# A transfer-bound matmul with adapted weights: first pair rounded by ScalarE, m merged earlier, half loads, an earlier first store, and idle waits on VectorE

## Chip, cores, metric

One core of a Trainium2 chip. The metric is device microseconds of a whole execution; medians are quoted with the lowest and highest run. The "span" is the part of an execution from its first to its last profiled instruction; it is a little shorter than the time.

## The reference

```python
batch, seq_len, in_dim, out_dim, rank = 16, 2048, 256, 256, 16
W_adapted = W + scale * (lora_A @ lora_B)
W_norm = np.sqrt(np.sum(W_adapted ** 2, axis=0, keepdims=True) + 1e-8)
W_final = W_adapted / W_norm * m
y = x.reshape(-1, in_dim) @ W_final          # 32768 x 256 in, 32768 x 256 out, float32
```

x and y are 33.6 MB each, the weights 0.3 MB. There is one matmul per row of x, so the work is mostly moving bytes.

## The kernel before

x is cut into 8 blocks of 4096 rows (4.19 MB, 32 KB per partition); five block buffers fit on the chip. A block is 8 chunks, two chunks are a pair. A pair goes: GpSimd rounds it to bf16, TensorE transposes it, VectorE copies the transposed pair out, TensorE multiplies it by w_final, ScalarE copies each chunk's result back *into the buffer of x*, and ScalarE's queue stores it. Loads go out on SyncE's queue (q1 in the profile), stores on ScalarE's (q10).

The parts that the change touches:

```python
loads = [(0, 2), (2, 2), (4, CH - 4)] + units[1 : XBUFS - 1]        # (first chunk, chunks)
loads += [((XBUFS - 1) * CH, CH - 3)]                               # chunks 32-36: 20 KB rows
loads += [(XBUFS * CH - 3 + c, 1) for c in range(3)] + units[XBUFS:]  # 37, 38, 39: 4 KB rows
...
stores = [(b * CH, CH, 21 + b) for b in range(F - 1)]               # (.., .., issued behind chunk)
stores += [(G - CH, CH // 2, 24), (G - CH // 2, CH // 2, 24)]
FIRST = len(stores)
stores += [(G + c, 1, G + 3) for c in range(4)]                     # 4 KB rows
stores += [(G + 4, CH - 4, 47)]
stores += [(b * CH, CH, max(47, (b + 1) * CH - 1)) for b in range(F + 1, NBLK - 1)]
...
# GpSimd: the first cast waits for dve 4; before pair REST it waits for half of block 2's store
if p == 0:
    nc.gpsimd.wait_ge(sem("dve"), 4)
if p == REST:
    nc.gpsimd.wait_ge(sem(f"store{HALF}"), 16)
...
for _ in range(IDLE):                       # 8, at the end of GpSimd's program
    nc.gpsimd.wait_ge(sem("ident"), 1)
...
# TensorE: norm's matmuls, then the one that spreads m over the partitions, then
turned(0)
nc.tensor.wait_ge(dv, 8)                    # w_final is there
nc.tensor.sem_inc(sem("room"), 2)           # two output buffers are free
with nc.Fori(0, NPR // 2, 1, engines=[PE], head_slot={PE: 128}):
    turned(1); product(0); turned(0); product(1)
```

## Time and profile before

| | before |
|---|---|
| time (first 3 runs) | 162.68 us (162.39 to 162.74) |
| span of the profiled run | 161.3 us |
| busiest compute engine | TensorE, 59% |
| bytes, mean rate | 67.42 MB, 418 GB/s |
| first store issued | 48.5 us |
| last arithmetic, last store issued | 131.2, 132 us |

The page and the table of stretches are shown in the prediction. In the table of stretches the columns are: the stretch and its length, busy time (and count) of each engine, the clock granted to TensorE (1 is full), DMA share, GB/s. In short stretches the last two are rough, since a packet counts by where it starts; where I give a loss in microseconds below, it is a sum over the trace's own DMA packet records, each packet's bytes spread over its duration, of how far half-microsecond slices under 424 GB/s fall short of 431. Such a loss comes from the one profiled run of a kernel, while times and mean spans come from all of its runs.

### The profile page before, as it was taken

To read this page: it belongs to the slowest core of one execution; us is meant where nothing else is said; L and a number is where in the kernel's file an instruction comes from. 1 tells how busy PE (TensorE), PEld (TensorE's weight loads), DVE (VectorE), ACT (ScalarE), POOL (GpSimd) and SP (SyncE) were. 2 spreads that over 40 slices of the span, in tenths; PEclk is the share of its full clock that TensorE was granted. 3 is DMA by queue.
4 is the path that set the end of the run, shared out by engine and by line. 5 is a ranking of instruction groups with operands and counts; after the bars stand their busy time and mean duration, and the time that the engine had idled before them with its cause. 6 is when DMAs were issued, how large, how long until landed. Compare 5 with 4: busy or idle time off the path is not lost. (4 is left out here: it accounts for less than half of the span.)

```text
span 161.3 us, 2012 instructions
## 1 busy us (share of the span) xinstructions
PE 95.2 (59%) x786; PEld 83.8 (52%) x786; DVE 46.6 (29%) x44; ACT 63.9 (40%) x67; POOL 62.9 (39%) x39
## 2 busy tenths in 40 slices
PE   0491899999999700000199999999999940000000
PEld 0160799999998600000179989989899930000000
DVE  0439635353635300000033535353445300000000
ACT  3010076868686520000027675856776850000000
POOL 1085339776764000000674479198676200000000
PEclk9999999999999995555559999999999998555555
DMA  4999999999899999989999999999999999999995
GB/s 163 427 455 459 390 504 406 390 488 423 374 412 361 511 423 390 473 374 451 427 482 414 386 463 421 407 433 433 422 484 419 406 479 414 400 479 423 386 443 228
DMA packets 4356, 67.42 MB, mean 418 GB/s; under 512 B 625, under 2 KB 642, under 8 KB 1666
## 3 DMA queue, kind: packets, MB, share of 16 engines
q1 hardware_dynamic: 2160, 33.82, 49.5%
q10 hardware_dynamic: 2194, 33.59, 48.7%
q14 instruction: 2, 0.02, 0.0%
HBM read 33.85 MB, written 33.55 MB: 418 GB/s over the span
## 5 line engine op out<-in xcount | busy, mean ns | idle before, releaser
L256 ACT COPY x_sb<-y_ps 128x1024 f32<-128x1024 f32 x64 | 62.0, 1014 | 60.0 <-PE y_ps L316 57.8
L197 POOL CAST xb<-x_sb 128x2048 bf16<-128x2048 f32 x32 | 60.4, 1900 | 61.3 <-DMA out_dram<-x_sb 27.7
L316 PE MATMUL y_ps<-w_final,xt 128*128 128x256 bf16 x512 | 63.6, 278 | 1.2 <-PEq L291 1.1
L238 DVE COPY xt<-xt_ps 128x1024 f32<-128x1024 f32 x32 | 39.2, 1224 | 72.6 <-PE xt_ps L302 72.6
L316 PEld LDWEIGHTS y_ps<-w_final,xt 128*128 128x128 bf16 x512 | 51.1, 100 | 8.5 <-issue 1.9
L302 PE MATMUL xt_ps<-identity,xb 128*128 128x128 f32 x264 | 37.0, 287 | 28.2 <-PEq L291 28.2
L302 PEld LDWEIGHTS xt_ps<-identity,xb 128*128 128x128 f32 x264 | 31.7, 148 | 30.3 <-issue 30.0
L283 PE MATMUL y_ps<-sq,ones 128*128 128x256 f32 x4 | 2.1, 674 | 1.6 <-DVE sq L223 1.6
L272 PE MATMUL y_ps<-identity,a_nat 128*16 128x128 f32 x2 | 0.6, 394 | 4.1 <-DMA a_nat<-in_lora_A_dram 4.1
L248 ACT ACTIVATE norm<-y_ps,eps_col 128x256 f32<-128x256 f32 x1 | 0.5, 473 | 5.8 <-PE y_ps L283 5.8
L234 DVE TENSOR_TENSOR w_final<-wam,rnorm 128x256 bf16<-128x256 f32 x2 | 2.5, 1266 | 0.0
L283 PEld LDWEIGHTS y_ps<-sq,ones 128*128 128x128 f32 x4 | 1.2, 326 | 2.3 <-DVE sq L223 2.1
L272 PEld LDWEIGHTS y_ps<-identity,a_nat 128*16 128x16 f32 x2 | 0.1, 88 | 4.1 <-issue 4.1
L246 ACT ACT_TABLE_LOAD x1 | 1.3, 1283 | 2.4 <-issue 2.4
L203 POOL MEMSET xb<- 128x2048 bf16 x1 | 1.8, 1804 | 0.7 <-PE xt_ps L302 0.7
L231 DVE RECIPROCAL rnorm<-norm 128x256 f32<-128x256 f32 x1 | 1.7, 1747 | 0.0
L225 DVE COPY m_all<-y_ps 128x256 f32<-128x256 f32 x1 | 0.4, 424 | 3.3 <-PE y_ps L288 3.3
L214 DVE CAST b_bf<-b_nat 16x256 bf16<-16x256 f32 x1 | 0.3, 281 | 3.5 <-DMA b_nat<-in_lora_B_dram 3.5
L288 PE MATMUL y_ps<-m_row,ones 1*128 1x256 f32 x2 | 1.2, 706 | 0.0
L276 PE MATMUL y_ps<-b_bf,aT 16*128 16x256 bf16 x2 | 0.6, 404 | 0.7 <-DVE aT L216 0.7
L219 DVE SCALAR_TENSOR_TENSOR wa<-y_ps,w_nat 128x512 f32<-128x512 f32 x1 | 0.7, 692 | 0.8 <-PE y_ps L276 0.8
L288 PEld LDWEIGHTS y_ps<-m_row,ones 1*128 1x128 f32 x2 | 0.5, 308 | 0.6 <-issue 0.6
(13 smaller groups left out, 3.3 us busy)
## 6 DMA issues: line engine op xcount, KB each, us to landing
x_sb<-in_x_dram SPq DMA_DIRECT2D x5, 4096.0 KB, 26.5
out_dram<-x_sb ACTq DMA_DIRECT2D x5, 4096.0 KB, 22.7
out_dram<-x_sb ACTq DMA_DIRECT2D x5, 2048.0 KB, 29.0
x_sb<-in_x_dram SPq DMA_DIRECT2D x3, 2048.0 KB, 31.4
x_sb<-in_x_dram SPq DMA_DIRECT2D x1, 2560.0 KB, 44.8
x_sb<-in_x_dram SPq DMA_DIRECT2D x2, 1024.0 KB, 6.1
out_dram<-x_sb ACTq DMA_DIRECT2D x4, 512.0 KB, 50.1
x_sb<-in_x_dram SPq DMA_DIRECT2D x3, 512.0 KB, 46.4
```

The lines of the kernel that those rows point to most:

```text
L197: nc.gpsimd.tensor_copy(out=xb_bufs[p % NXB][:], in_=x_bufs[b % XBUFS][:, 2 * c * J : 2 * (c + 1) * J, :],).then_inc(sem("rounded"), 1)
L203: nc.gpsimd.memset(xb_bufs[NPR % NXB][:], 0.0).then_inc(sem("rounded"), 1)
L219: nc.vector.scalar_tensor_tensor(out=wa[:], in0=ab_ps, scalar=float(scale), in1=w_nat[:], op0=ALU.mult, op1=ALU.add).then_inc(dv, 1)
L231: nc.vector.reciprocal(out=rnorm[:], in_=norm[:]).then_inc(dv, 1)
L234: i = nc.vector.tensor_mul(out=w_final[:, t], in0=wam[:, t], in1=rnorm[:])
L238: nc.vector.tensor_copy(out=xt_bufs[p % NXT][:].rearrange("p r t -> p (r t)").bitcast(FP32), in_=xt_ps[p % 2][:],).then_inc(sem("copied"), 1)
L246: nc.scalar.activation(out=warm[:], in_=eps_col[:], func=AF.Sqrt)
L256: nc.scalar.copy(out=x_bufs[b % XBUFS][:, c * J : (c + 1) * J, :], in_=y_ps[g % 2][:]).then_inc(sem("room"), 1)
L283: i = nc.tensor.matmul(n2_ps, ones[:], sq[:, t, :], start=(t == 0), stop=(t == KC - 1))
L288: nc.tensor.matmul(mb_ps, ones[0:1, :], m_row[:], start=True, stop=True).then_inc(pe, 1)
L302: i = nc.tensor.transpose(xt_ps[p % 2][:, j * P : (j + 1) * P], xb_bufs[p % NXB][:, j, :].bitcast(FP32), identity[:],)
L316: i = nc.tensor.matmul(y_ps[h][:, j, :], xt_bufs[p % NXT][:, r : r + P, t], w_final[:, t, :], start=(t == 0 and (j % (J // 2)) == 0), stop ...
```

## The change

Its intent: start computing earlier (m merged before the norm is ready, ScalarE rounds the first pair, GpSimd kept off VectorE's port while w_final is made), wait less for loads (half loads), and begin the stores earlier (behind chunk 19). Idle waits on VectorE were added to those on GpSimd. The core of the diff:

```diff
+    loads = [(0, 2, 2 * J), (2, 2, 2 * J)] + [(g0, 4, 4 * J) for g0 in range(4, 24, 4)]
+    loads += [(24, CH, CH * J), (H - CH, 5, 5 * J), (H - 3, 3, J)]
+    loads += [(H, CH, CH * J)] + [(g0, 4, 4 * J) for g0 in range(H + CH, NCH, 4)]
+    stores = [(b * CH, CH, CH * J, 19 + b) for b in range(F - 1)]
+    stores += [(G - CH, 4, 4 * J, G - 1), (G - 4, 4, 4 * J, G - 1)]
+    stores += [(G, 4, J, G + 3), (G + 4, CH - 4, (CH - 4) * J, 48)]      # pieces share a semaphore
 ... (GpSimd)
-        if p == 0:
-            nc.gpsimd.wait_ge(sem("dve"), 4)
+        if p == 1:
+            nc.gpsimd.wait_ge(sem("dve"), 6)
+        if p == 2:
+            nc.gpsimd.wait_ge(sem("dve"), 8)
 ... (VectorE)
-    nc.vector.wait_ge(sem("pe"), 4)
+    nc.vector.wait_ge(sem("pe"), 3)
     nc.vector.tensor_copy(out=m_all[:], in_=mb_ps).then_inc(dv, 1)
 ...
+    nc.vector.wait_ge(dv, 8)
+    nc.vector.sem_inc(sem("room"), 2)
 ...
     for _ in range(IDLE):
         nc.gpsimd.wait_ge(sem("ident"), 1)
+        nc.vector.wait_ge(sem("ident"), 1)
 ... (ScalarE)
+    wait_load(nc.scalar, 0)
+    nc.scalar.copy(out=xb_bufs[0][:], in_=x_bufs[0][:, 0 : 2 * J, :]).then_inc(sem("early"), 1)
 ... (TensorE: m's matmul moves ahead of the norm's)
-    nc.tensor.wait_ge(dv, 8)
-    nc.tensor.sem_inc(sem("room"), 2)
```

More of the change, by code (lines that the diff above doesn't have):

```diff
@@ L103, with pieces @@
     units += [(NCH - CH, CH // 2), (NCH - CH // 2, CH // 2)]
-    loads = [(0, 2), (2, 2), (4, CH - 4)] + units[1 : XBUFS - 1]
-    loads += [((XBUFS - 1) * CH, CH - 3)]
-    loads += [(XBUFS * CH - 3 + c, 1) for c in range(3)] + units[XBUFS:]
-    load_of = {g: n for n, (g0, cnt) in enumerate(loads) for g in range(g0, g0 + cnt)}
     F = NBLK - XBUFS
     G = F * CH
-    stores = [(b * CH, CH, 21 + b) for b in range(F - 1)]
-    stores += [(G - CH, CH // 2, 24), (G - CH // 2, CH // 2, 24)]
-    FIRST = len(stores)
-    stores += [(G + c, 1, G + 3) for c in range(4)]
-    stores += [(G + 4, CH - 4, 47)]
-    stores += [(b * CH, CH, max(47, (b + 1) * CH - 1)) for b in range(F + 1, NBLK - 1)]
-    stores += [(g0, cnt, g0 + cnt - 1) for g0, cnt in units[-2:]]
-    HALF = FIRST - 2
+    H = XBUFS * CH
+    loads = [(0, 2, 2 * J), (2, 2, 2 * J)] + [(g0, 4, 4 * J) for g0 in range(4, 24, 4)]
+    loads += [(24, CH, CH * J), (H - CH, 5, 5 * J), (H - 3, 3, J)]
+    loads += [(H, CH, CH * J)] + [(g0, 4, 4 * J) for g0 in range(H + CH, NCH, 4)]
+    load_of = {g: n for n, (g0, cnt, _) in enumerate(loads) for g in range(g0, g0 + cnt)}
+    stores = [(b * CH, CH, CH * J, 19 + b) for b in range(F - 1)]
+    stores += [(G - CH, 4, 4 * J, G - 1), (G - 4, 4, 4 * J, G - 1)]
+    FIRST = len(stores)
+    stores += [(G, 4, J, G + 3), (G + 4, CH - 4, (CH - 4) * J, 48)]
+    stores += [(b * CH, CH, CH * J, max(48, (b + 1) * CH - 1)) for b in range(F + 1, NBLK - 1)]
+    stores += [(g0, cnt, cnt * J, g0 + cnt - 1) for g0, cnt in units[-2:]]
+    def pieces(entry):
+        return 16 * (entry[1] * J // entry[2])
     late = [nc.alloc_semaphore(f"store{n}") for n in range(FIRST, len(stores))]
@@ L132, in sem, with transfer, wait_load, wait_store @@
         return sems[name]
-    def in_sbuf(g0, cnt):
+    def transfer(engine, name, entry, dram, store):
+        g0, cnt, rows = entry[:3]
         b, c = divmod(g0, CH)
-        return x_bufs[b % XBUFS][:, c * J : (c + cnt) * J, :]
-    def in_dram(dram, g0, cnt):
         (u0, ucnt), = [u for u in units if u[0] <= g0 < u[0] + u[1]]
         unit = dram[u0 * J * P : (u0 + ucnt) * J * P].rearrange("(p j) k -> p j k", p=P)
-        return unit[:, (g0 - u0) * J : (g0 - u0 + cnt) * J, :]
+        for r in range(0, cnt * J, rows):
+            here = x_bufs[b % XBUFS][:, c * J + r : c * J + r + rows, :]
+            there = unit[:, (g0 - u0) * J + r : (g0 - u0) * J + r + rows, :]
+            src, dst = (here, there) if store else (there, here)
+            engine.dma_start(out=dst, in_=src).then_inc(sem(name), 16)
     def load_x(n):
-        nc.sync.dma_start(
-            out=in_sbuf(*loads[n]), in_=in_dram(x_flat, *loads[n])
-        ).then_inc(sem(f"load{n}"), 16)
+        transfer(nc.sync, f"load{n}", loads[n], x_flat, False)
     def store_y(n):
-        nc.scalar.dma_start(
-            out=in_dram(out_flat, *stores[n][:2]), in_=in_sbuf(*stores[n][:2])
-        ).then_inc(sem(f"store{n}"), 16)
+        transfer(nc.scalar, f"store{n}", stores[n], out_flat, True)
+    def wait_load(engine, g):
+        engine.wait_ge(sem(f"load{load_of[g]}"), pieces(loads[load_of[g]]))
+    def wait_store(engine, n):
+        engine.wait_ge(sem(f"store{n}"), pieces(stores[n]))
     nc.sync.dma_start(
@@ L162 @@
     for n in range(len(loads)):
-        if loads[n][0] == XBUFS * CH:
-            for k in range(HALF + 1):
-                nc.sync.wait_ge(sem(f"store{k}"), 16)
-        if loads[n] == units[-1]:
-            nc.sync.wait_ge(sem(f"store{HALF + 1}"), 16)
+        if loads[n][0] == H:
+            for k in range(FIRST - 1):
+                wait_store(nc.sync, k)
+        if loads[n][0] == H + G - 4:
+            wait_store(nc.sync, FIRST - 1)
         load_x(n)
@@ L183 @@
     ).then_inc(sem("ident"), 1)
-    for p in range(NPR):
+    for p in range(1, NPR):
         b, c = divmod(p, PRB)
         for g in (2 * p, 2 * p + 1):
-            if g == 0 or load_of[g - 1] != load_of[g]:
-                nc.gpsimd.wait_ge(sem(f"load{load_of[g]}"), 16)
-        if p == 0:
-            nc.gpsimd.wait_ge(sem("dve"), 4)
+            if g == 2 or load_of[g - 1] != load_of[g]:
+                wait_load(nc.gpsimd, g)
+        if p == 1:
+            nc.gpsimd.wait_ge(sem("dve"), 6)
+        if p == 2:
+            nc.gpsimd.wait_ge(sem("dve"), 8)
         if p == REST:
-            nc.gpsimd.wait_ge(sem(f"store{HALF}"), 16)
+            wait_store(nc.gpsimd, FIRST - 2)
         if p >= NXB:
@@ L203 @@
     nc.gpsimd.memset(xb_bufs[NPR % NXB][:], 0.0).then_inc(sem("rounded"), 1)
-    for _ in range(IDLE):
-        nc.gpsimd.wait_ge(sem("ident"), 1)
     dv = sem("dve")
@@ L241 @@
         ).then_inc(sem("copied"), 1)
+    for _ in range(IDLE):
+        nc.gpsimd.wait_ge(sem("ident"), 1)
+        nc.vector.wait_ge(sem("ident"), 1)
     nc.scalar.wait_ge(dv, 1)
     nc.scalar.activation(out=warm[:], in_=eps_col[:], func=AF.Sqrt)
-    nc.scalar.wait_ge(sem("pe"), 3)
+    wait_load(nc.scalar, 0)
+    nc.scalar.copy(out=xb_bufs[0][:], in_=x_bufs[0][:, 0 : 2 * J, :]).then_inc(
+        sem("early"), 1
+    )
+    nc.scalar.wait_ge(sem("pe"), 4)
     nc.scalar.activation(
@@ L258 @@
         ).then_inc(sem("room"), 1)
-        due = [n for n in range(len(stores)) if stores[n][2] == g]
+        due = [n for n in range(len(stores)) if stores[n][3] == g]
         if due:
@@ L279 @@
     i.then_inc(pe, 1)
+    nc.tensor.wait_ge(sem("load_m"), 16)
+    nc.tensor.matmul(mb_ps, ones[0:1, :], m_row[:], start=True, stop=True).then_inc(pe, 1)
     nc.tensor.wait_ge(dv, 4)
@@ L286 @@
     i.then_inc(pe, 1)
-    nc.tensor.wait_ge(sem("load_m"), 16)
-    nc.tensor.matmul(mb_ps, ones[0:1, :], m_row[:], start=True, stop=True).then_inc(pe, 1)
     def take(name):
@@ L298, in turned @@
     def turned(p):
-        take("rounded")
         for j in range(2 * J):
@@ L323, in product @@
             i.then_inc(sem("product"), 1)
+    nc.tensor.wait_ge(sem("early"), 1)
     turned(0)
-    nc.tensor.wait_ge(dv, 8)
-    nc.tensor.sem_inc(sem("room"), 2)
     with nc.Fori(0, NPR // 2, 1, engines=[PE], head_slot={PE: 128}):
+        take("rounded")
         turned(1)
         product(0)
+        take("rounded")
         turned(0)
@@ L338 @@
     tc.compile()
-    for s in late:
-        nc.sync.wait_ge(s, 16)
+    for k, s in enumerate(late):
+        nc.sync.wait_ge(s, pieces(stores[FIRST + k]))
         nc.sync.sem_clear(s)
```

## The prediction

> **What bounds the kernel now.** I read the page's slices first, then the table of stretches, then the chain of waits, and only then the timeline of the head.
>
> The page (busy time of PE, the DMA slices, the queues):
>
> ```profile
> PE 95.2 (59%) x786; PEld 83.8 (52%) x786; DVE 46.6 (29%) x44; ACT 63.9 (40%) x67; POOL 62.9 (39%) x39
> DMA  4999999999899999989999999999999999999995
> GB/s 163 427 455 459 390 504 406 390 488 423 374 412 361 511 423 390 473 374 451 427 482 414 386 463 421 407 433 433 422 484 419 406 479 414 400 479 423 386 443 228
> DMA packets 4356, 67.42 MB, mean 418 GB/s; under 512 B 625, under 2 KB 642, under 8 KB 1666
> q14 instruction: 2, 0.02, 0.0%
> ```
>
> No compute engine is over 59% busy, while the DMA row is full except in the first and the last slice. The 67.42 MB are compulsory: x once in, y once out, plus the small weights. The table of stretches gives the rate that counts as full:
>
> ```profile
> core 0: us, PE busy (x) PEld busy (x) DVE busy (x) ACT busy (x) POOL busy (x), PEclk, DMA share, GB/s
> 0.00:3.00 3.00, 0.00 (x0) 0.00 (x0) 0.17 (x2) 0.59 (x1) 0.70 (x6) 1.00 0.25 58
> 3.00:43.00 40.00, 32.45 (x244) 27.64 (x245) 19.45 (x20) 18.52 (x21) 22.82 (x12) 1.00 1.01 432
> 43.00:49.50 6.50, 6.50 (x62) 6.01 (x61) 3.67 (x3) 4.42 (x6) 5.01 (x3) 1.00 0.99 418
> 49.50:52.50 3.00, 2.90 (x28) 2.48 (x26) 1.22 (x1) 2.40 (x3) 0.67 (x1) 1.00 1.02 340
> 52.50:78.00 25.50, 3.12 (x28) 2.42 (x25) 1.22 (x1) 3.19 (x4) 0.12 (x1) 0.66 1.01 435
> 78.00:110.00 32.00, 29.46 (x245) 26.45 (x246) 12.25 (x10) 18.63 (x20) 21.95 (x12) 0.89 1.01 432
> 110.00:158.00 48.00, 20.82 (x189) 18.78 (x187) 8.57 (x7) 16.17 (x17) 11.64 (x7) 0.77 1.00 431
> 158.00:161.30 3.30, 0.00 (x0) 0.00 (x0) 0.00 (x0) 0.00 (x0) 0.00 (x0) 0.50 0.44 189
> ```
>
> Last column: 432 GB/s with loads alone (3 to 43 us), 435 with stores alone (52.5 to 78), 432 with both (78 to 110). So it doesn't matter to the rate which way the bytes go. The time is start-up (about 2.6 us lost in 0:3), 67.42 MB / 432 GB/s = 156.1 us, and a tail (3.3 us at 189 GB/s, so 1.9 us lost). That makes 160.6 of the 161.3 us. The one other hole is 49.5 to 52.5 us: 340 GB/s although the DMA share says 1.02, so the engines are occupied but slow. It costs 3.0 x (432-340)/432 = 0.64 us.
>
> The chain of waits shows the same thing from the other end; its last two pieces are
>
> ```profile
> 130.19 1.01 ACT x_sb L256
> 131.21 0.92 ACTq L262
> ```
>
> The last arithmetic ends at 131.2 us, the last store is issued about 132, and 29 us of stores queued before it still have to drain. Even the middle is elastic; from the list of waits:
>
> ```profile
> POOL xb L197 <- DMA out_dram<-x_sb: 27.7, 1, 27.7
> ```
>
> GpSimd stands 27.7 us by design, until a store has landed, and no byte is moved later for it.
>
> **What the Trainium skill says.** "DMA: Bandwidth & Descriptors", section "Where 436 GB/s comes from", puts the ceiling of the 16 ports at 435.2 GB/s. The trace agrees (432 to 435 above); the same section's HBM limit of about 358 per core doesn't bind here, and the measurement decides. The same page, "Queues, rings and completion order", says that each DMA engine takes turns between queue rows packet by packet. The trace agrees: between 84 and 100 us, with 32 KB load rows (q1) beside 4 KB store rows (q10), the queues moved
>
> ```profile
> q1 hardware_dynamic: 207, 6.26, 90.6%
> q10 hardware_dynamic: 207, 0.78, 11.9%
> ```
>
> exactly as many packets each, so the row size sets the share. "SBUF — State Buffer", section "SBUF: two separate sides", says that VectorE operations with two SBUF inputs and GpSimd operations that read SBUF lock each other out of a shared port pair. The head of the timeline agrees:
>
> ```profile
> 11.30 0.76 DVE L228 TENSOR_TENSOR wam<-wa,m_all 128x256 f32<-128x256 f32 x2
> 11.97 1.75 DVE L231 RECIPROCAL rnorm<-norm 128x256 f32<-128x256 f32 x1
> 13.76 2.45 DVE L234 TENSOR_TENSOR w_final<-wam,rnorm 128x256 bf16<-128x256 f32 x2
> 13.82 2.11 POOL L197 CAST xb<-x_sb 128x2048 bf16<-128x2048 f32 x1 [2.43 <-DMA x_sb<-in_x_dram]
> ```
>
> The two products for w_final take 2.45 us under a GpSimd cast, the same operation for wam took 0.76 with GpSimd idle.
>
> **The change, part by part.** (1) The head. The matmul that spreads m moves ahead of the norm's matmul, so VectorE's copy of m and wam (0.42 + 0.76 us) are done by about 8.8 us, while TensorE sums squares. The reciprocal can start when the norm is ready (9.69 + 0.47 = 10.2 us, was 11.97): 1.8 us earlier. GpSimd's third cast must now wait for w_final, so its two products should take about 0.8 us, not 2.45: 1.7 us more. ScalarE rounds the first pair meanwhile (2,048 elements at twice the 1,014 ns of its 1,024-element copies, about 2 us, from 6.6 us on), before the norm needs it. w_final is then ready about 12.7 us instead of 16.2, and the first product starts near 14.3 us instead of 18.6: about 4 us earlier.
>
> (2) Half loads. Compute runs at 2.62 us per pair of chunks, so 10.5 us per block, beside 9.7 us per load; it stood idle for blocks 1 and 2 (2.8 and 1.4 us before the casts). Halves land about 4.9 us earlier for their first rows, so these waits mostly go.
>
> (3) First store behind chunk 19, one pair (2.62 us) before 21. With (1) and (2) it should be issued about 40 to 43 us instead of 48.5. At 41 us some (41-2.6) x 0.432 = 16.6 of the 21.3 MB of the first loads are in. So the three 4 KB-row loads (chunks 37 to 39), which now run alone from 48 to 53 us, will run beside 32 KB store rows. What this is worth: by the trace's own packet records, which I summed because no view prints them, their 384 packets take 183 ns on average when alone (up to 220 late in the hole), and the 4 KB stores beside big loads take 159. (183-160) x 384 / 16 engines = 0.55 us, the same hole as the 0.64 us above. This is the gain.
>
> (4) The price of halves: blocks 1, 2 and 6 go from 384 packets of 32 KB (1,214 ns by the same records) to 768 of 16 KB (611 ns). 384 x (1222-1214) / 16 = 0.19 us, and about 0.03 us for three more completions.
>
> (5) The idle waits for VectorE stand at the end of a program that has 30 us to spare: 0. They can only shift when instructions are fetched (two packets on q14); the records show each at 0.31 us on one DMA engine, so at most some 0.3 us in the tail.
>
> So the 4 us of the head and all compute gains lie under the DMA and are worth nothing directly; they only bring the first store forward. Sum: -0.55 to -0.64 + 0.22 = about -0.35 us: 162.68 becomes 162.3. I say 162.35, as the hole may not close fully.
>
> **The rivals.** (a) The DMA runs dry in the middle. Before the second group of stores, which now waits for chunk 48, only all loads (33.85 MB) and 3.5 blocks of stores (14.68 MB) exist: 48.5 MB, or about 2.6 + 112.3 = 115 us. Before, chunk 47 released the group at 110.85 us, with GpSimd 3.25 us idle for block 6. Now its first half comes some 5 us sooner; I expect 107 to 110 us. A spare of 5 us speaks against it. If the group came as late as 120, the loss would be 4 to 5 us (167).
>
> (b) Early stores choke the first loads: 32 KB store rows against 20 KB and 4 KB load rows leave these 38% and 11% of the engines. Chunks 32 to 39 then land at 60 us and later. But GpSimd stands at chunk 30 until the first half of block 2 is stored (about 76 to 78 us) anyway, so it is hidden: 0, at worst 1 us.
>
> (c) The gain of 4 us at the head carries to the end: about 158.7. Against it speak the 29 us of queued stores.
>
> (d) The tail. The 16 engines end together only if they share work evenly; in the completion counts of the last store the median engine lands at 160.0 us and the last at 161.2. A longer mixed phase can change this by 0.5 us either way, the largest doubt in my range.
>
> **Range and chances.** 162.35, and 8 times in 10 within 161.7 to 163.1: the lower end has the hole closed, the price zero and a tail 0.3 shorter, the upper end no gain, the full price and a tail 0.3 longer. The runs before spread over 0.35 us. A gain of 2% (3.25 us) would need more than all that is lost at the hole and the tail together: 1%. A loss of 2% needs rival (a): 2%. Within 2%: 97%.
>
> **What would show it.** Right: bytes unchanged, all stretches from 3 to 158 us at 430 or more with no 340 left; first store issued near 41 us, and stores in the packets while loads still run; w_final near 12.7 us with its two products under 1 us; the second group issued before 112 us; the last arithmetic some us before 131, or as late, without effect. Wrong: a stretch of a microsecond or more with a low DMA share around 110 to 120 us (rival a), a slow stretch that has merely moved to other 4 KB rows, or a tail much over 1.9 us lost (rival d).

## The result, and the profile after

| | before | after |
|---|---|---|
| time | 162.43 us (162.24 to 162.74, 6 runs) | 163.57 us (163.27 to 163.90, 6 runs) |
| ratio | | 1.0069 (1.0053 to 1.0086) |
| span of the profiled run | 161.3 us | 162.0 us |
| time less span, mean | 1.29 to 1.31 us in every group of runs | 1.64 us |

The change made the kernel 1.1 us slower; the prediction was 0.35 us faster, with 163.1 as the upper end. From the page after:

```profile
PE 95.3 (59%) x786; PEld 84.7 (52%) x786; DVE 45.0 (28%) x44; ACT 65.9 (41%) x68; POOL 60.9 (38%) x38
DMA  4999999999899999999999999999999999999995
DMA packets 4788, 67.42 MB, mean 416 GB/s; under 512 B 673, under 2 KB 690, under 8 KB 1714
```

The same bytes, the same engines, the same full DMA row. The table of stretches after has the slow stretch in another place:

```profile
3.00:40.00 37.00, 32.64 (x245) 28.06 (x246) 17.96 (x21) 20.60 (x22) 20.80 (x11) 0.95 1.01 432
...
44.50:48.50 4.00, 3.29 (x30) 3.14 (x31) 1.23 (x1) 2.33 (x3) 4.00 (x3) 1.00 1.03 345
48.50:78.00 29.50, 4.76 (x44) 4.09 (x42) 2.45 (x2) 4.47 (x5) 0.25 (x1) 0.62 1.01 430
...
118.00:158.00 40.00, 14.11 (x130) 12.85 (x127) 5.43 (x5) 11.56 (x12) 6.82 (x4) 0.70 1.00 432
158.00:162.00 4.00, 0.00 (x0) 0.00 (x0) 0.00 (x0) 0.00 (x0) 0.00 (x0) 0.50 0.51 217
```

345 GB/s from 44.5 to 48.5 us. The hole was not closed, it went along with the first store. The timelines of ScalarE's queue have that store's issue, before:

```profile
48.53 0.37 ACTq L149 DMA_DIRECT2D out_dram<-x_sb  x1
```

and after:

```profile
42.80 0.37 ACTq L145 DMA_DIRECT2D out_dram<-x_sb  x1
```

In both kernels the loads slow down about 2 us after this issue and stay slow for about 2 us, until the first packets of the store appear (52.6 us before, 47.1 after). The stretches before and after:

```profile
50.50:52.50 2.00, 1.90 (x18) 1.50 (x17) 1.22 (x1) 1.77 (x2) 0.00 (x0) 1.00 1.01 305
```

```profile
45.00:47.00 2.00, 1.79 (x17) 1.72 (x18) 0.69 (x1) 0.93 (x1) 2.00 (x3) 1.00 0.83 215
```

By the packet records the stretch cost 0.69 us before and 0.95 after: after, it fell among loads with 20 KB rows, whose packets took 877 ns on average instead of 766, while the 4 KB rows now took 160 as predicted.

The head did what the prediction said. Timeline after:

```profile
6.59 1.90 ACT L261 CAST xb<-x_sb 128x2048 bf16<-128x2048 f32 x1 [2.72 <-DMA x_sb<-in_x_dram]
10.19 1.75 DVE L235 RECIPROCAL rnorm<-norm 128x256 f32<-128x256 f32 x1 [1.29 <-ACT norm L265]
11.98 0.76 DVE L238 TENSOR_TENSOR w_final<-wam,rnorm 128x256 bf16<-128x256 f32 x2
13.90 3.74 POOL L205 CAST xb<-x_sb 128x2048 bf16<-128x2048 f32 x2 [2.96 <-DMA x_sb<-in_x_dram]
14.45 3.23 PE L332 MATMUL y_ps<-w_final,xt 128*128 128x256 bf16 x16 [2.12 <-PEq L308]
```

w_final is ready at 12.74 us (predicted 12.7, before 16.2) because its two products take 0.76 us with GpSimd held back (2.45 before), and the first product starts at 14.45 us (predicted 14.3, before 18.6). None of it reaches the end. The list of waits and the chain after:

```profile
POOL xb L205 <- DMA out_dram<-x_sb: 29.9, 1, 29.9
```

```profile
131.27 1.01 ACT x_sb L273
132.28 0.92 ACTq L279
```

GpSimd gives 2.2 us of its lead back at the store that it waits for by design (27.7 us before), and the last arithmetic comes a microsecond later than before, with 29 us of stores still to drain.

Two numbers are to be explained, then: 0.7 to 0.8 us more in the span, and about 0.35 us more outside it.

### The profile page after: what moved, and what is told of

It is laid out like the page before. It is cut to its first block, busy times and chain, and to the rows that moved or that the text cites. A ratio compares the mean times of both kernels' runs of the same rounds, so it can differ in the third digit from the quotient of the medians.

```text
span 162.0 us, 2018 instructions
## 1 busy us (share of the span) xinstructions
PE 95.3 (59%) x786; PEld 84.7 (52%) x786; DVE 45.0 (28%) x44; ACT 65.9 (41%) x68; POOL 60.9 (38%) x38
## 2 busy tenths in 40 slices
DMA packets 4788, 67.42 MB, mean 416 GB/s; under 512 B 673, under 2 KB 690, under 8 KB 1714
## 3 DMA queue, kind: packets, MB, share of 16 engines
q1 hardware_dynamic: 2592, 33.82, 49.6%
q10 hardware_dynamic: 2194, 33.59, 48.4%
## 5 line engine op out<-in xcount | busy, mean ns | idle before, releaser
L205 POOL CAST xb<-x_sb 128x2048 bf16<-128x2048 f32 x31 | 58.4, 1896 | 64.3 <-DMA out_dram<-x_sb 29.9
L332 PE MATMUL y_ps<-w_final,xt 128*128 128x256 bf16 x512 | 64.3, 281 | 3.2 <-PEq L308 3.2
L318 PEld LDWEIGHTS xt_ps<-identity,xb 128*128 128x128 f32 x264 | 32.4, 150 | 29.7 <-issue 29.1
L261 ACT CAST xb<-x_sb 128x2048 bf16<-128x2048 f32 x1 | 1.9, 1899 | 2.7 <-DMA x_sb<-in_x_dram 2.7
L232 DVE TENSOR_TENSOR wam<-wa,m_all 128x256 f32<-128x256 f32 x2 | 0.8, 422 | 0.0
```

What stands on the lines that cost most here:

```text
L205: nc.gpsimd.tensor_copy(out=xb_bufs[p % NXB][:], in_=x_bufs[b % XBUFS][:, 2 * c * J : 2 * (c + 1) * J, :],).then_inc(sem("rounded"), 1)
L261: nc.scalar.copy(out=xb_bufs[0][:], in_=x_bufs[0][:, 0 : 2 * J, :]).then_inc(sem("early"), 1)
L318: i = nc.tensor.transpose(xt_ps[p % 2][:, j * P : (j + 1) * P], xb_bufs[p % NXB][:, j, :].bitcast(FP32), identity[:],)
L332: i = nc.tensor.matmul(y_ps[h][:, j, :], xt_bufs[p % NXT][:, r : r + P, t], w_final[:, t, :], start=(t == 0 and (j % (J // 2)) == 0), stop ...
```

## The experiments

Theories at the start. *Inside the span:* the loss belongs to the first store and moves with it, larger among larger load rows; rivals: the half loads cost it, or it is a price of first touching the output, or the 4 KB rows are slow by themselves, as I had predicted. *Outside the span:* the idle waits on VectorE; rival: they are free.

All results in one table. "First store" is the issue of the first one in the profiled run (in e4 of the first big one), "loss there" the loss at that store, "later" the losses at later places where loads and stores meet. Rows marked * have no slow stretch at the first store; their 0.18 or 0.19 is only the three loads with 4 KB rows, which run alone at some 408 GB/s.

| kernel | first store us | loss there | later | span, mean of runs | time less span | ratio to before |
|---|---|---|---|---|---|---|
| before | 48.5 | 0.69 | 0.05 | 161.1 to 161.3 | 1.29 to 1.31 | 1 |
| after | 42.8 | 0.95 | 0 | 161.95 | 1.64 | 1.0069 |
| e1 | 43.0 | 1.09 | 0 | 161.9 | 1.56 | 1.0059 (1.0045 to 1.0073) |
| e2 | 45.3 | 1.29 | 0 | 161.9 | 1.62 | 1.0056 (1.0042 to 1.0069) |
| e3 | 47.9 | 0.92 | 0 | 161.3 | 1.44 | 1.0010 (0.9997 to 1.0023) |
| e4 | 48.4 | 0.90 | 0 | 161.5 | 1.30 | 1.0011 (0.9998 to 1.0024) |
| e5 | 45.3 | 1.04 | 0.20 | 161.75 | 1.31 | 1.0029 (1.0012 to 1.0045) |
| e6* | 49.6 | 0.18 | 0.29 | 161.2 | 1.57 | 1.0015 (0.9997 to 1.0034) |
| e7 | 47.6 | 0.70 | 0 | 161.25 | 1.30 | 0.9994 (0.9978 to 1.0010) |
| e8 | 21.1 | 0.19 | 0.79 | 161.55 | 1.31 | 1.0017 (1.0000 to 1.0034) |
| e9* | 49.8 | 0.18 | 0.49 | 161.3 | 1.56 | 1.0025 (1.0011 to 1.0039) |
| e10* | 49.6 | 0.19 | 0.65 | 161.6 | 1.30 | 1.0032 (1.0009 to 1.0055) |
| e11* | 50.9 | 0.18 | 1.15 | 161.8 | 1.59 | 1.0052 (1.0037 to 1.0066) |
| e12 | 42.5 | 0.99 | 0 | 161.8 | 1.65 | 1.0061 (1.0046 to 1.0077) |
| e13* | 49.5 | 0.19 | 0.48 | 161.3 | 1.57 | 1.0030 (1.0014 to 1.0046) |
| e14 | 48.1 | 0.85 | 0 | 161.3 | 1.31 | 1.0014 (0.9999 to 1.0029) |
| e15 | 46.1 | 0.92 | 0 | 161.8 | 1.30 | 1.0042 (1.0029 to 1.0056) |
| e16* | 49.6 | 0.19 | 0.46 | 161.1 | 1.32 | 1.0000 (0.9985 to 1.0015) |
| e17 | 42.6 | 1.02 | 0 | 162.0 | 1.31 | 1.0053 (1.0039 to 1.0067) |

### First group: idle waits, whole loads, an early touch of the output

**e1**, the changed kernel without VectorE's idle waits:

```diff
     for _ in range(IDLE):
         nc.gpsimd.wait_ge(sem("ident"), 1)
-        nc.vector.wait_ge(sem("ident"), 1)
```

> The changed kernel without VectorE's eight idle waits. Theory A (the waits move an instruction fetch to the end of the program; it shows as a packet after the span, and as 1.67 us between the time and the span instead of 1.29): the time falls by about 0.4 us to 163.15, ratio to before 1.0045, the span stays at 162.0, the late instruction packet is gone. Rival (waits at the end of a stream are free, as the prediction said): no change, 163.55, ratio 1.007.

Time less span fell from 1.64 to 1.56, not to 1.29. The instruction packet after the span did go, so that packet is not what holds the time up by 0.4 us.

**e3**, the kernel before with these waits:

```diff
         ).then_inc(sem("copied"), 1)
+    for _ in range(IDLE):
+        nc.vector.wait_ge(sem("ident"), 1)
```

> The kernel before with the eight idle waits on VectorE added, nothing else. Theory A: 0.4 us slower, about 162.85, ratio 1.0025, the span stays 161.3, an instruction packet after the span. Rival: 162.45, ratio 1.000.

1.44 against 1.31: 0.13 us outside the span, a third of what I expected, and no late instruction packet at all. So the waits cost about 0.1 us, and most of the 0.35 us was still unexplained.

**e2**, the changed kernel with blocks 1, 2 and 6 loaded whole:

```diff
-    loads = [(0, 2, 2 * J), (2, 2, 2 * J)] + [(g0, 4, 4 * J) for g0 in range(4, 24, 4)]
-    loads += [(24, CH, CH * J), (H - CH, 5, 5 * J), (H - 3, 3, J)]
-    loads += [(H, CH, CH * J)] + [(g0, 4, 4 * J) for g0 in range(H + CH, NCH, 4)]
+    loads = [(0, 2, 2 * J), (2, 2, 2 * J), (4, 4, 4 * J)]
+    loads += [(g0, CH, CH * J) for g0 in range(CH, H - CH, CH)]
+    loads += [(H - CH, 5, 5 * J), (H - 3, 3, J)]
+    loads += [(H, CH, CH * J), (H + CH, CH, CH * J)]
+    loads += [(g0, 4, 4 * J) for g0 in range(H + 2 * CH, NCH, 4)]
```

> The changed kernel with blocks 1, 2 and 6 loaded whole again (32 KB rows). Theory (16 KB rows cost 8 ns more per 32 KB): 0.2 us faster, span about 161.8, ratio about 1.0055; block 3 lands about 0.14 us earlier. Rival (the halves are what makes the stores collide with the loads): the slow stretch at the first store (20 KB load packets at 877 ns on average against 766) vanishes, and over 0.5 us come back, ratio under 1.004. Waiting for whole blocks moves the first store back by some 3 us, so that its size in the slow stretch is seen beside other packets as well.

The expected 0.2 us did not show in the span, which is the same. It is there in the records of the loads: block 3 lands 0.30 us earlier than in the changed kernel (42.72 against 43.02, median of the 16 completions). But the loss at the first store was the largest of all, 1.29 us, and ate it up. The rival falls too: the stretch did not vanish with the halves.

**e4**, the kernel before with a small early store:

```diff
+    early = out_flat[0 : CH * J * P].rearrange("(p j) k -> p j k", p=P)
+    nc.scalar.dma_start(out=early[:, 0, 0:P], in_=ones[:]).then_inc(sem("early_store"), 16)
     nc.scalar.activation(out=warm[:], in_=eps_col[:], func=AF.Sqrt)
 ...
+                if n == 0:
+                    nc.scalar.wait_ge(sem("early_store"), 16)
                 store_y(n)
```

> The kernel before with a small store (512 bytes per partition, 64 KB, overwritten later) issued at about 2.5 us. Theory W (the slow stretch of 340 GB/s is a one-time cost of the first write to HBM, so it can be paid early for 64 KB): the 4 KB loads around 50 us take 160 ns instead of 183, the stretch from 49.5 to 52.5 us runs at 430, and the time falls by 0.4 to 0.6 us, to 161.9, ratio 0.9965. Theory C (any start of stores beside running loads costs it): the stretch stays at about 340, and the time rises by 0.1 to 0.2 us for the extra bytes, ratio 1.001.

The slow stretch stayed; one line of its table of stretches:

```profile
50.50:52.50 2.00, 1.93 (x19) 1.53 (x17) 1.22 (x1) 1.89 (x2) 0.00 (x0) 1.00 0.98 262
```

Having written to the output once, with 64 KB, is not what the first big store lacks.

### Second group: each part of the change on the kernel before

**e5**, only the early stores:

```diff
-    stores = [(b * CH, CH, 21 + b) for b in range(F - 1)]
-    stores += [(G - CH, CH // 2, 24), (G - CH // 2, CH // 2, 24)]
+    stores = [(b * CH, CH, 19 + b) for b in range(F - 1)]
+    stores += [(G - CH, CH // 2, G - 1), (G - CH // 2, CH // 2, G - 1)]
```

> The kernel before with the first three stores due at chunks 19, 20 and 23 (was 21, 22, 24), nothing else. The first store should go out near 45.9 us, with 20 KB load rows in flight. Theory L (a slow stretch of about 2 us begins some 2 us after the first large store is issued, and costs more with 20 KB load packets in flight than with 4 KB ones): load packets lose 0.9 to 1.2 us per engine (before: 0.6 to 0.75), span +0.3 to +0.4, time 162.9, ratio about 1.002. Rival (the size in flight doesn't matter; the larger loss of the changed kernel is chance or comes with the halves): 0.6 to 0.75 lost, ratio 1.000.

As the theory has it. The issue and the stretch after it:

```profile
45.31 0.37 ACTq L149 DMA_DIRECT2D out_dram<-x_sb  x1
```

```profile
47.50:49.50 2.00, 1.90 (x18) 1.50 (x17) 1.22 (x1) 1.92 (x2) 1.83 (x1) 1.00 0.87 229
```

1.04 us lost there, the span 0.4 us longer than before in the same rounds (161.75 against 161.33), time less span untouched. This also takes away the prediction's reason for the hole: here the slow packets have 20 KB rows.

**e6**, only the new head (and the row pieces on shared semaphores): the changed kernel with the loads of e2, no idle waits on VectorE, and

```diff
-    stores = [(b * CH, CH, CH * J, 19 + b) for b in range(F - 1)]
-    stores += [(G - CH, 4, 4 * J, G - 1), (G - 4, 4, 4 * J, G - 1)]
+    stores = [(b * CH, CH, CH * J, 21 + b) for b in range(F - 1)]
+    stores += [(G - CH, 4, 4 * J, 24), (G - 4, 4, 4 * J, 24)]
-    stores += [(G, 4, J, G + 3), (G + 4, CH - 4, (CH - 4) * J, 48)]
+    stores += [(G, 4, J, G + 3), (G + 4, CH - 4, (CH - 4) * J, 47)]      # and max(48, ..) to max(47, ..)
```

> The changed kernel with its loads, stores due and idle waits set back to those of the kernel before: what is left is the new head and the row pieces that share one semaphore. My account: nothing in the span except by way of the first store, which comes some 2 us earlier, so it falls among 20 KB rows: span 161.2 to 161.6. The time less the span is 1.31 before, 1.67 after, and the idle waits account for 0.13: if the new head or the shared semaphores carry the rest, it is 1.5 here; if not, 1.3. Ratio 1.001 to 1.004.

The span is that of before, and 0.26 us are added outside it: the head, or the shared semaphores, carry what the idle waits don't (e9 tells them apart). I was wrong on the first store, which came later (49.6 us), not earlier, and then met no slow stretch.

**e7**, only the half loads:

```diff
-    loads = [(0, 2), (2, 2), (4, CH - 4)] + units[1 : XBUFS - 1]
+    loads = [(0, 2), (2, 2)] + [(g0, 4) for g0 in range(4, 24, 4)] + [(24, CH)]
-    loads += [(XBUFS * CH - 3 + c, 1) for c in range(3)] + units[XBUFS:]
+    loads += [(XBUFS * CH - 3 + c, 1) for c in range(3)] + [units[XBUFS]]
+    loads += [(g0, 4) for g0 in range((XBUFS + 1) * CH, NCH, 4)]
```

> The kernel before with blocks 1, 2 and 6 in half loads, nothing else. By packet sizes +0.19 us in the span, ratio 1.0012, if the first store then still meets 4 KB rows; it may come 1 to 3 us sooner, since the waits for blocks 1 and 2 go, and then the loss beside 20 KB rows adds 0.3: ratio 1.003. Rival (halves are what costs): 1.005 or more. The time less the span should stay 1.3.

Nothing that the clock can show: 0.9994. The interval just excludes the predicted 1.0012, but the landing times in the changed kernel have the cost: block 3 lands 0.22 us later than before (43.02 against 42.80), of which 0.08 are there already at the first load, so 0.14 for two halved blocks; 0.13 was predicted for two. All seven kernels with half loads show it: from 4 to 42 us their loads fall 0.10 to 0.18 us behind 431 GB/s, those of the others by at most 0.04 (e8, which stores early, left out). Block 6 adds 0.06 on average (84 to 113 us). That makes 0.2 us, too little for the clock to tell from noise here.

**e8**, the kernel before with the first pair stored at once:

```diff
-    stores = [(b * CH, CH, 21 + b) for b in range(F - 1)]
+    stores = [(0, 2, 1), (2, CH - 2, 21)] + [(b * CH, CH, 21 + b) for b in range(1, F - 1)]
```

> The kernel before with chunks 0 and 1 stored as a small first store (1 MB in 8 KB rows) as soon as they are computed, about 23 us; the rest of block 0 as before at chunk 21. Theory O (the loss is paid once per execution by the first store of real size, while loads run): a slow stretch some 2 us after that store, near 25 us, and none at 50 us; the time within 0.3 us of before. Theory P (the loss comes each time when stores start beside loads after a time without stores): two slow stretches, +0.5 to +0.9 us, ratio 1.003 to 1.006.

The small store cost 0.19 us, the big one 28 us later still cost its full 0.79:

```profile
51.50:53.50 2.00, 1.93 (x19) 1.51 (x17) 1.23 (x1) 1.90 (x2) 0.00 (x0) 1.00 1.01 281
```

So it is not paid once by any store of real size. The ratio, 1.0017, is lower than the 1.003 that I gave theory P.

### Third group: later stores, smaller rows

**e9**, e6 with each piece on its own semaphore:

```diff
-    loads += [(H - CH, 5, 5 * J), (H - 3, 3, J)]
+    loads += [(H - CH, 5, 5 * J)] + [(H - 3 + c, 1, J) for c in range(3)]
-    stores += [(G, 4, J, G + 3), (G + 4, CH - 4, (CH - 4) * J, 47)]
+    stores += [(G + c, 1, J, G + 3) for c in range(4)]
+    stores += [(G + 4, CH - 4, (CH - 4) * J, 47)]
```

> The head-alone kernel with each 4 KB row piece on its own load or store semaphore again (as in the kernel before), so that only the new head is left. The head-alone kernel had a time 1.57 us longer than its span, the kernel before 1.31. If the shared semaphores carry the 0.26, it is 1.31 here and the ratio falls by 0.0016; if the head carries it, it stays 1.57.

1.56: not the semaphores.

**e10**, the kernel before with its first store one chunk later:

```diff
-    stores = [(b * CH, CH, 21 + b) for b in range(F - 1)]
+    stores = [(b * CH, CH, 22 + b) for b in range(F - 1)]
```

> The kernel before with its first store one chunk later (22 and 23 instead of 21 and 22), so issued near 49.8 us, as in the head-alone kernel, which showed no slow stretch. Theory L (a slow stretch only where loads still run 2 us after the issue): the 4 KB load packets lose under 0.2 us instead of 0.58 to 0.75, span 160.8 to 161.0 and time 162.1, ratio 0.997: the fastest version so far. Rival (the slow stretch in the kernels timed has nothing to do with the issue): ratio 1.000.

The first stretch went as expected:

```profile
49.50:51.50 2.00, 1.89 (x18) 1.54 (x17) 1.22 (x1) 1.02 (x2) 0.05 (x1) 1.00 1.02 408
```

The time didn't follow: ratio 1.0032, with spans of 161.0, 161.0, 161.4, 162.0, 162.0 and 162.2. In the profiled run, one of the two with 161.0, losses had come up where the second group of stores meets the last loads:

```profile
114.00:116.00 2.00, 2.00 (x21) 1.87 (x20) 0.14 (x1) 1.93 (x2) 0.88 (x2) 1.00 0.92 328
```

What the longer runs did I can't say, as they left no trace. The hoped-for faster version isn't one.

**e11**, the changed kernel with its first stores held back:

```diff
-    stores = [(b * CH, CH, CH * J, 19 + b) for b in range(F - 1)]
-    stores += [(G - CH, 4, 4 * J, G - 1), (G - 4, 4, 4 * J, G - 1)]
+    stores = [(b * CH, CH, CH * J, G) for b in range(F - 1)]
+    stores += [(G - CH, 4, 4 * J, G + 1), (G - 4, 4, 4 * J, G + 1)]
```

> The changed kernel with its first stores held back to chunk 24 (and 25), so issued near 50.5 us, when the first loads are nearly in; all else as changed. If the early store is the main loss inside the span: load packets lose under 0.2 us instead of 0.9, span about 161.1, time about 162.75, ratio 1.001, with what is left being the 0.36 us outside the span. Rival (the loss comes from the halves, the head or the mixed phase): stays above 1.005.

A miss: 1.0052, where 1.001 was expected. The first stretch was gone, but where block 5 begins to load beside the stores there was a new one:

```profile
81.00:82.50 1.50, 1.50 (x9) 1.09 (x8) 1.01 (x1) 0.00 (x0) 1.19 (x2) 0.50 1.03 289
```

0.85 us there and 0.30 more around 116 us. Here it is the *stores* that slow down, before the first packet of a *load* appears. So the loss isn't the first store's own: in these traces it stands where one stream starts beside the other, and when the first such meeting is spared, a later one can pay.

**e12**, the changed kernel with the first store in 4 KB rows:

```diff
-    stores = [(b * CH, CH, CH * J, 19 + b) for b in range(F - 1)]
+    stores = [(b * CH, CH, J if b == 0 else CH * J, 19 + b) for b in range(F - 1)]
```

> The changed kernel with its first store cut into eight pieces with 4 KB rows instead of 32 KB rows, on the same semaphore and at the same moment. If the row size of the incoming store makes the slow stretch (a 1 MB store with 8 KB rows cost only about 0.2 us): 20 KB load packets lose 0.1 to 0.3 us instead of 0.9 to 1.05. If it does not matter: 0.9 again. The 4 KB rows cost 0.47 us by themselves (1,024 packets at 159 ns instead of 128 at 1,213), so the ratio is 1.004 in the first case and 1.009 in the second.

Those 4 KB packets came in at 46.0 us without a slow stretch, but from 47 us on, when more of the stores came, it was there all the same:

```profile
47.00:49.50 2.50, 1.54 (x13) 1.21 (x14) 0.40 (x1) 2.01 (x3) 1.60 (x1) 1.00 0.98 323
```

20 KB load packets lost 0.56 us, between the two cases that I had set; the whole stretch, drawn out to 63 us, lost 0.99. Small rows don't avoid it.

### Fourth group: what was still open

**e13** and **e14**, e9 with one instruction more or less on TensorE and VectorE:

```diff
 e13                                              e14
+    for _ in range(2):                           -    nc.vector.wait_ge(dv, 8)
+        nc.tensor.sem_inc(sem("spare"), 1)       -    nc.vector.sem_inc(sem("room"), 2)
     with nc.Fori(...)                            +    nc.tensor.wait_ge(dv, 8)
                                                  +    nc.tensor.sem_inc(sem("room"), 2)
                                                       with nc.Fori(...)
```

> The new head alone with two spare semaphore instructions on TensorE ahead of its loop, so that as many instructions stand before the loop as in the kernel before. If the 0.26 us that the head adds outside the span comes from where TensorE's program stands in its fetch blocks, the time less the span falls from 1.56 to about 1.30; if not, it stays 1.56.

> The new head alone with the wait for w_final and the count of free output buffers moved back from VectorE to TensorE: VectorE then has as many instructions as before, TensorE one fewer than before. If the 0.26 us comes from VectorE's program, 1.30; if from TensorE's or ScalarE's, 1.56 (or in between).

1.57 and 1.31. The 0.26 us outside the span come with the pair of the wait and the semaphore increment that the change put on VectorE; with them back on TensorE the new head costs nothing there. Why a step at 13 us should lengthen what follows the span, no run shows.

**e15**, half loads and early stores together on the kernel before (the edits of e7 and e5, added lines of blocks 1 and 2 and of the stores only):

```diff
+    loads = [(0, 2), (2, 2)] + [(g0, 4) for g0 in range(4, 24, 4)] + [(24, CH)]
+    stores = [(b * CH, CH, 19 + b) for b in range(F - 1)]
+    stores += [(G - CH, CH // 2, G - 1), (G - CH // 2, CH // 2, G - 1)]
```

> The kernel before with half loads and the first stores at chunks 19, 20 and 23 together; its head, semaphores and idle waits unchanged. If the two parts add up (each alone gave +0.3 and 0.0 in the span): span 161.6, time 162.95, ratio 1.002 to 1.003. If together they cost more than apart, which is what the changed kernel's span of 161.9 suggests: span 161.8 to 162.0, ratio 1.004 to 1.005. The time less the span stays 1.30.

Ratio 1.0042, mean span 161.80 against 161.13 before: the whole 0.7 us of the span, without the new head, the shared semaphores or the idle waits. Together they cost more than apart (1.0029 and 0.9994), though the intervals are too wide to say by how much. The loss at the first store, 0.92 us, is only 0.23 more than before; the rest is in the loads' own rate and in the tail (see below).

**e16**, the kernel before without GpSimd's idle waits:

```diff
-    IDLE = 8
+    IDLE = 0
```

> The kernel before without the eight idle waits on GpSimd. Span unchanged (161.2 to 161.4). If such waits only set how long the core needs after its span, the time less the span moves away from 1.30, by 0.1 us or more in either direction; if they do nothing, 1.30.

1.32 and a ratio of 1.0000: on GpSimd they do nothing that can be seen. In its profiled run the first store went out 1.1 us later than in the profile of before, behind the same chunk 21, and found no slow stretch:

```profile
49.61 0.37 ACTq L149 DMA_DIRECT2D out_dram<-x_sb  x1
```

```profile
49.50:52.00 2.50, 2.50 (x26) 2.33 (x24) 1.10 (x2) 1.29 (x3) 1.75 (x1) 1.00 1.02 405
```

**e17**, the changed kernel with e1's and e14's edits, so with its loads, stores and the rest of its head:

```diff
-        nc.vector.wait_ge(sem("ident"), 1)
-    nc.vector.wait_ge(dv, 8)
-    nc.vector.sem_inc(sem("room"), 2)
+    nc.tensor.wait_ge(dv, 8)
+    nc.tensor.sem_inc(sem("room"), 2)
```

> The changed kernel with both suspects of the time outside the span undone: no idle waits on VectorE, and the count of free output buffers raised by TensorE instead of VectorE. Loads, stores and the rest of the head as changed. If the account is right, the time less the span falls from 1.67 to 1.31 while the span stays at 161.9: time 163.2, ratio 1.0042, the same as the kernel before with half loads and early stores (1.0042). If the two parts don't add up, 1.4 to 1.6 stay.

1.31, as expected: the loss outside the span is gone to the last tenth. The span is 162.0, so the ratio, 1.0053, is a little above the 1.0042 that I expected; its interval holds it.

## Why the prediction was wrong, point by point

**What bounds the kernel** was right: 67.42 MB at full rate, everything else hidden. So were the steps of the head (w_final, first product, first store at 42.8 within 40 to 43), the price of the half loads' packets (0.14 us for two blocks and 0.06 for block 6, 0.19 predicted), rival (a) not happening (48.5 to 158 us at 427 to 434 GB/s in the profile after, though the second group of stores came at 112.8, later than the 107 to 110 that I gave), and rival (b) being hidden.

**The step that failed is (3).** It read the hole at 49.5 to 52.5 us as "4 KB rows that run alone", with 183 ns against 159, and took its closing as the gain: "This is the gain." The records that I averaged would have shown otherwise, taken in order of time: from 48.2 to 50.5 us the 4 KB loads ran just as alone and took 162 ns on average, none over 172; from 50.5 us on, 2 us after the store's issue, they took 210 on average and up to 502 (the "up to 220 late in the hole" was an average too). The average mixed two stages. Running alone costs the 4 KB rows at most 0.18 us (the rows marked *), not 0.55. What the runs showed in its place: of the 19 kernels, the twelve that issued their first store at 48.6 us or sooner (and e8, whose first big store went out at 49.4 us) lost 0.7 to 1.3 us there; the six that issued it at 49.5 us or later lost nothing there beyond the 0.18 us of the 4 KB rows, but 0.29 to 1.15 us at later places. The change moved the store from the edge of this range well into it. (e16, the kernel before but for idle waits of GpSimd, is on the other side in its profile; the kernel before itself has only one.) So instead of gaining 0.55 to 0.64 us the first store lost more than before: 0.26 us in the profiled pair, 0.35 in e5's profile, whose span is 0.4 us longer. The prediction's own sign of being wrong came close: it named a slow stretch that moves to other 4 KB rows; this one moved to 20 KB rows.

The rest of the span's 0.7 us is not at the first store. How far the bytes of the two profiled runs fall behind 431 GB/s, over all slices, tells where it is:

| stretch of the span | before | after | more |
|---|---|---|---|
| up to 4 us | 2.69 | 2.74 | 0.05 |
| 4 to 42 us, loads (blocks 1 and 2 in halves after) | 0.00 | 0.17 | 0.17 |
| 42 to 55 us, the first store begins | 0.70 | 0.95 | 0.25 |
| 55 to 158 us (block 6 in halves after) | -0.07 | 0.04 | 0.11 |
| 158 us to the end | 1.52 | 1.67 | 0.15 |

In the prediction's terms: the gain of 0.55 to 0.64 was a loss of 0.25, and the price of the halves, 0.22, came out at about 0.2 (the seven kernels under e7). This is one run of each kernel, and the last line, the tail, varies from 1.24 to 1.89 us over the 19 profiles, so 0.15 there can be chance.

**Step (5) failed too.** It looked for the waits' cost only in the tail of the span, and the prediction silently took time less span, 1.29 us in the profiled run, as a constant. It isn't: VectorE's idle waits add 0.1 (e1, e3; in e3 without any late instruction packet, so a moved fetch is not all that such waits can do), and the wait and semaphore increment on VectorE, which I had not priced at all, 0.26 (e9, e14). The sum, 0.7 + 0.1 + 0.26, is the 1.1 us measured, and e17 takes the last two away.

**Rival (d)**, the tail, explains at most the 0.15 us in the table: in the completion counts of the last store the last engine lands 1.41 us behind the median, against 1.26. Its spread over the profiles bears out that it was the largest doubt.

**Open:** why streams that start beside each other stall for some 2 us, why a first meeting with a loss leaves later ones with little or none, and why a meeting that is spared can be paid for later (e10, e11). The engines are nearly in step before the stretch (the 16 completions of one load lie 0.25 us apart, first to last) and out of step at the load that lands after it (2.7 us apart before, 2.4 after), so it may be the price of falling out of step, but no run tests that. Which part of VectorE's extra instructions acts outside the span, and how, is open as well.

## What to carry to other kernels

Where the DMA is always full, an earlier start of the stores need not gain anything, and it can lose. Starting the second stream when the first was nearly through spared the loss there, but no kernel here became measurably faster by it, since the loss came back elsewhere: measure whole runs. Before a slow average is put down to the size of the packets, look at the packets in order of time and ask what was issued just before (here 2 us). And compare time with span in every run: a tenth or a quarter of a microsecond can hide outside of everything that a profile shows.

## What the Trainium skill lacked or had wrong

- "DMA: Bandwidth & Descriptors", section "Queues, rings and completion order", describes the turns that queues take packet by packet, and the trace agrees (207 packets each). It has nothing on what the start of a second stream costs: here mostly 0.7 to 1.3 us for streams of 32 KB rows, in stretches of 2 us or so at 50 to 71% of 431 GB/s (215 to 305), mostly before the new stream's first packet is seen.
- The same page, section "Latency and other measured facts", gives some 600 ns to the first byte for transfers issued by SyncE or ScalarE. The first load here took about 1.0 us from issue to first packet, the first big store 3.6 to 4.7 us beside running loads, and 1.4 to 2.5 us where they were about to end.
- No page that I found has the time outside the profiled span as something that a kernel's own instructions change: 1.29 to 1.32 us in ten of these kernels, 1.44 with eight idle waits on VectorE (e3), 1.56 to 1.57 with one more wait and semaphore increment there instead (e1, e6, e9, e13), 1.59 to 1.65 with both.
